# Attention scores in 128-row matmuls: a zero-padded query tile for the low-part product, and a split in two parts for group C of the second layer

## The chip, the cores and the metric

One core of one Trainium2 chip runs the whole program. The metric is the device time of one execution in microseconds; for the kernel before it is the median of three runs. The engines are TensorE (PE in the profile, PEld for its weight loads), VectorE (DVE), ScalarE (ACT), GpSimd (POOL) and SyncE (SP).

## The reference, cut to what matters

Two transformer layers over 256 latent and 256 context tokens, then a third block (recurrent mixer, cross attention, feed-forward) on the latent tokens. Everything is float32. Each of the two layers has three groups of attention heads; the change touches their scores.

```python
def attention(q, k, v, bias_or_mask, sink):          # for every head
    s = einsum('qd,kd->qk', q, k) * scale + bias_or_mask
    p = softmax(concat([s, sink]))                    # sink: group B only
    return p @ v
# group A: 8 heads of 64 columns, neighbourhood bias on the latent keys
# group B: 12 query heads, 4 key heads of 64 columns, band mask, a sink
# group C: 6 heads of 192 columns: 128 wide ones (keys from a low-rank product)
#          and 64 with rotary embedding, shared by the heads on the key side
# latent queries read 512 keys (latent and context), context queries 256 (context)
# layer 1: queries of both streams; layer 2: latent queries only
```

## The kernel before

**Parts and products.** A float32 value is kept as two float32r parts, a high and a low one, each exact in a one-pass product. An input product is the sum of three one-pass products, high x high, low x high, high x low (lines 416 to 418, and 436 to 439 for transposed results). Weights come from DRAM as raw tiles (`raw`, on SP's queue), ACT makes the high part (line 372) and DVE the low part (line 373). Products of plain float32 operands are also possible; they take several passes.

**Scores of 64 columns.** For groups A and B and for the rotary columns of group C, `stacked` transposes the queries of a pair of heads and puts, for each head, the high part in one half of the 128 partitions and the low part in the other half (`Q`). For the keys it puts the high part in both halves (`KK`), and the low parts of the two heads of a pair in the two halves of a tile of its own (`KL`). One product over 128 rows then gives (high + low) x high; a second one, over the 64 rows of the head's half alone, adds high x low. In the trace these two are `Ss<-k,q` (128 rows) and `Ss<-kl,q` (64 rows), both at line 525 in `scores`.

**Group C.** Its 128 wide columns are transposed by `toT`. With `parts=1` the result is one float32 tile (`T`), copied by ACT or DVE (`copy`, lines 360 to 368), and the wide part of a score is one float32 product `Ss<-T,T`. With `parts=2`, `toT` calls `split_scaled`: ACT writes the high part, DVE the low part, and `job_c` makes three one-pass products. `nparts = 1, 1` chooses one part in both layers.

**Jobs.** `scores` writes one PSUM bank for one head and 128 queries; DVE adds bias or mask and takes the maximum (lines 530, 532), ACT makes the exponentials (line 536), `divide` scales them (line 546), `turn` transposes them on PE (line 553) and `values` multiplies them with the values (line 568, out of a pair's four score tiles). These are stages of a job: `first`, `part`, `second`, `end`. `job_ab` and `job_c` push the jobs; for group A's latent queries a stage `load` ahead of `first` fetches the bias on SP's queue and POOL adds a mask to it (line 992).

**Order.** The stages run between the steps of the input and output products. `tick` counts microseconds of PE's work; `serve` starts a new job every `every` = 2.0 of them, and a number between two stages (`soft`, `lag`, `lag2`, `ahead`) is the least distance between them. Norms of heads are `urgent` work: a square on ACT, a sum on DVE, a power on POOL (`rstd`, line 351), then the scaling. The rotary embedding ends in an addition on POOL (line 729). DVE also has side work in layer 1, sums for the modulation vectors (line 664, `ada_steps`). The framework orders the instructions of an engine by when they can run and by the order in which they were written; each engine then goes through its list in order.

**Memory.** 50 tiles `U` of 128x512 hold activations; 40 tiles of 16 columns hold small sums (`small`). A tile `cs` holds constants for the whole program; its last 256 columns, `tri` and `stri`, are used by the third block alone (`exps`, line 1514).

Of the kernel before, what the change touches and what calls it, by code (L numbers as in the profile page):

```python
# [25 lines left out]
# per-partition vectors: name -> (first column, columns)  # L26
# [25 lines left out]
# constants that depend on shapes alone: name -> (first column, columns)  # L52
# [13 lines left out]
def flip():  # L66
    """reverses 64 by 64"""
    p = np.arange(128)
    return ((p[:, None] // 64 == p[None] // 64) & (p[:, None] % 64 == 63 - p[None] % 64)).astype(np.float32)
# [28 lines left out]
# weights as blocks of two k-tiles [128, 2 x columns] in the order of their use: name -> (rows, chunks), a chunk  # L98
# being [(first column, columns)] side by side
# [20 lines left out]
# shift and scale of the first layer: (first k-tile, k-tiles) of the parts that are worked out one after another  # L120
# [12 lines left out]
def packed_ada(w):  # L133
    """the parts of PARTS as [k-tile, 128, shift and scale]; then the gate of the first layer, shift and scale and the
    gate of the second as [quarter of the channels, block, 128 columns, 512 channels]"""
# [7 lines left out]
class Weights:  # L143
    """a packed weight in DRAM"""
# [14 lines left out]
class Act:  # L159
    """Transposed activations [channel, token] as two float32r parts, 512 // T k-tiles to a unit; make(u) works  # L160
    out unit u when it is first needed (or one unit ahead of that)."""
# [21 lines left out]
class Pair:  # L183
    """Token tiles 0, 1 of one and 2, 3 of another."""
# [8 lines left out]
class K:  # L193
    # microseconds of the tensor engine: between the starts of two jobs, two urgent stages, two stages of a job; between
    # the halves of a norm, from norms to transposes, from these to the jobs; from scores to the division, to the
    # transposes, to the values; from the load of a bias to the scores
    every, spaced, gap = 2.0, 0.65, 1.3
    settle, hold, after, soft, lag, lag2, ahead, split_lag, unit_lag = 4.0, 6.5, 2.5, 1.2, 2.5, 3.0, 2.5, 1.2, 2.0
    nparts = 1, 1

    def __init__(self, ctx, tc, a):
# [14 lines left out]
        self.cs = self.const.tile([128, NCS], F32, name="cs")  # L216
        nc.scalar.dma_start(self.cs, a["cst"])
# [9 lines left out]
    # ---- tiles  # L227
# [4 lines left out]
    def c(self, name):  # L232
        a, n = CS[name]
        return self.cs[:, a:a + n]
# [11 lines left out]
    def B(self, name, tag=None, bufs=2, cols=512, dt=F32):  # L246
        """a tile of the pool of the part at hand"""
        return self.bp.tile([128, cols], dt, name=self.name(name), tag=tag or name, bufs=bufs)
# [5 lines left out]
    def small(self, n=16):  # L254
        return self.sm.tile([128, 16], F32, name=self.name("sm"), tag="s", bufs=40)[:, :n]

    # ---- work that runs beside the products: jobs of several stages (a number is a delay after the stage before it),
    # or a number alone, before the next start),
    # which start one after another when the urgent work that was there before them is done
# [3 lines left out]
    def urge(self, f, ts, then=()):  # L263
        """f(t), a generator that yields once, for all ts, then the stages then; before the jobs that follow"""
# [11 lines left out]
    def free(self):  # L276
        """whether the next job may start"""
# [33 lines left out]
    def defer(self, dt, f):  # L311
        """f, which waits for another engine's work, dt later"""
        self.late.append((self.now + dt, f))

    def catch_up(self, all=True):
        """before what needs deferred work"""
# [28 lines left out]
    # ---- elementwise helpers  # L345
    def rstd(self, ss, n, count):
        """(ss / count + eps) ** -0.5 for [128, n]"""
# [6 lines left out]
    def copy(self, out, in_, scale=None):  # L354
        """to SBUF on ScalarE and VectorE by turns; scale: an AP [128, 1] or a number"""
# [14 lines left out]
    def split(self, hi, lo, src):  # L370
        """src = hi + lo, each exact in a float32r product"""
# [9 lines left out]
    # ---- products with weights from DRAM  # L381
# [3 lines left out]
    def weights(self, w, k0, pieces):  # L385
        """two k-tiles from k0 of a chunk of w: [(hi, lo)] tiles [128, <=512]"""
# [12 lines left out]
    def dense(self, act, kts, w, pieces, cols, evac, what="d", skip={}):  # L399
        """out[token, n] = act^T w for the token tiles cols, without the first skip[t] columns for tile t;  # L400
        evac(col, psum) or, for these, evac(col, psum, skip[t])"""
# [21 lines left out]
    def denseT(self, act, w, pieces, evac, what="e"):  # L423
        """out[n, token] = w^T act, tiles of 128 columns n, 512 // T to a bank; evac([bank])"""
# [18 lines left out]
    # ---- transposed activations  # L443
# [11 lines left out]
    def unit(self, T, ks, src, gain=None, rb=None, shift=None, new=None):  # L455
        """src(kt, t) -> AP [128 tokens, 128]; (hi, lo) of the transposed k-tiles ks, times gain(kt, stream) and
        the row rb, plus shift(kt, stream)"""
# [31 lines left out]
    def row(self, pt, t, r):  # L489
        """pt[p, t * 128 + i] = r[i] in every partition, for r: [128, 1]"""  # L490
# [3 lines left out]
    def rows(self, r, out):  # L494
        """r: [128, 1] of each token tile -> out[p, t * 128 + i] = r[t][i] in every partition"""
# [6 lines left out]
    def normT(self, X, gain, shift=None, ss=None, rb=None):  # L502
        """X[t][n]: [128, 512] tiles -> rms-normed, scaled and shifted, transposed; ss: their sums of squares;
        rb: the reciprocal norms as from rows()"""
# [13 lines left out]
    # ---- softmax attention  # L518
    def scores(self, qk, nk, mask=None, sink=None):
        """exponentials of the scores of one head and 128 queries, [128, nk], for divide"""  # L520
# [28 lines left out]
    def turn(self, P, nk, PT, q):  # L549
        """P transposed into PT[key pair][:, key, q*128..]"""  # L550
# [10 lines left out]
    def values(self, parts, nk):  # L561
        """parts: [(first output partition, PT, value tiles [128 keys, d])] -> psum [d.., 256 queries]"""
# [1340 lines left out]
```

## Time and profile before

| | |
|---|---|
| median of 3 runs | 3569.3 us (3567.42 to 3569.88) |
| span of the profiled execution | 3557.0 us |
| between the two | 12.3 us |
| PE busy | 3458.7 us (97%) |
| PE weight loads busy | 2943.2 us (83%) |
| DVE busy | 2295.3 us (65%) |
| ACT busy | 1787.8 us (50%) |
| POOL busy | 264.0 us (7%) |
| mean granted clock of TensorE | 0.989 of full |

The span runs from the first to the last instruction of the one execution that was profiled; the time of a run has what lies around it too. Busy shares are means over parts of the program with different limits. Layer 1's attention lies between 269 and 1000 us, layer 2's between 1278 and 1723 us, and the third block follows. A matmul's printed duration reaches into that of the next, so for PE the distance between two starts tells more than the duration.

### The profile page before, as it was taken

What the parts mean: (1) busy time and instruction counts of PE and PEld (TensorE: products, weight loads), DVE (VectorE), ACT (ScalarE), POOL (GpSimd) and SP (SyncE); (2) the same over time, 40 slices, a digit from 0 to 9 for tenths busy, and PEclk for the clock granted to TensorE, in tenths of its full rate; (3) what the DMA queues carried; (4) which work ended last, traced back from release to release, by engine and by line L of the source; (5) the groups of instructions that cost most, each with busy time, mean ns of one, the idle gap of its engine ahead of it and who ended that gap; (6) DMA issues with size and microseconds to landing.
All of it is one profiled execution on the core that took longest, in us unless ns stands there. A gap on an engine that the chain in (4) does not pass through costs nothing.

```text
span 3557.0 us, 56978 instructions
## 1 busy us (share of the span) xinstructions
PE 3458.7 (97%) x20830; PEld 2943.2 (83%) x20830; DVE 2295.3 (65%) x4925; ACT 1787.8 (50%) x3552; POOL 264.0 (7%) x315
## 2 busy tenths in 40 slices
PE   8999999999999999999999999999999899999998
PEld 3467767888777878788777999999988899999886
DVE  2359888867876555877664555555566766666554
ACT  3235555426525454666564445544555555555544
POOL 0011101101111011101110000000000000000000
PEclk9999999999999999999999999999999999999999
DMA  7645443662365434444554535555654455555665
GB/s 253 229 146 169 123 132 116 189 191 74 125 210 177 156 111 134 156 129 146 168 160 132 188 119 188 182 183 183 202 190 160 138 184 183 184 184 181 204 194 166
DMA packets 226729, 590.44 MB, mean 166 GB/s; under 512 B 39888, under 2 KB 63168, under 8 KB 226448
## 3 DMA queue, kind: packets, MB, share of 16 engines
q1 hardware_dynamic: 221104, 570.41, 50.3%
q0 software_dynamic: 4816, 15.56, 1.4%
q8 instruction: 163, 2.67, 0.3%
q14 instruction: 118, 0.97, 0.1%
q10 hardware_dynamic: 528, 0.84, 0.1%
HBM read 582.48 MB, written 4.24 MB: 165 GB/s over the span
## 4 chain that ended last, share of the span: by engine, by line
PE 91%; DVE 4%; ACT 1%; DMA 1%; issue 1%; POOL 1%; POOLq 0%; DVEq 0%; ACTq 0%; SPq 0%
PE upd L438 5%; PE upd L436 5%; PE upd L439 5%; PE Ss L525 3%; PE downd L418 2%; PE downd L417 2%; PE downd L416 2%; PE oo L568 2%; PE adao L625 2%; PE pTt L553 2%; PE L0zd L439 2%; PE L0zd L436 2%; PE L0zd L438 2%; PE L0outd L416 2%; PE L0outd L417 1%; PE L0outd L418 1%
## 5 line engine op out<-in xcount | busy, mean ns | idle before, releaser
L373 DVE TENSOR_TENSOR lo<-raw,hi 128x512 fp32r<-128x512 f32 (+3 forms) x1788 | 1200.9, 677 | 892.8 <-ACT hi L372 882.7
L372 ACT ACTIVATE hi<-raw 128x512 fp32r<-128x512 f32 (+3 forms) x1788 | 1089.4, 614 | 1314.9 <-DVE lo L373 214.6
L436 PE MATMUL upd<-hi,hi 128*128 128x256 f32 x1408 | 399.7, 284 | 0.0
L438 PE MATMUL upd<-lo,hi 128*128 128x256 f32 x1408 | 399.6, 284 | 0.0
L439 PE MATMUL upd<-hi,lo 128*128 128x256 f32 x1408 | 399.4, 284 | 0.0
L664 DVE SCALAR_TENSOR_TENSOR scr<-raw,cb 128x512 f32<-128x512 f32 x448 | 298.8, 695 | 26.2 <-DMA raw<-in_w_ada_dram 13.9
L438 PEld LDWEIGHTS upd<-lo,hi 128*128 128x128 f32 x1408 | 271.1, 193 | 0.3 <-DVE lo L480 0.3
L439 PEld LDWEIGHTS upd<-hi,lo 128*128 128x128 f32 x1408 | 271.1, 193 | 0.0
L436 PEld LDWEIGHTS upd<-hi,hi 128*128 128x128 f32 x1408 | 271.1, 193 | 0.0
L351 POOL TENSOR_TENSOR sm<-sm,mhalf 128x2 f32<-128x2 f32 (+4 forms) x116 | 116.4, 1006 | 1693.9 <-DVE sm L350 1656.5
L418 PE MATMUL downd<-hi,lo 128*128 128x512 f32 x352 | 137.0, 389 | 0.0
L417 PE MATMUL downd<-lo,hi 128*128 128x512 f32 x352 | 137.0, 389 | 0.0
L416 PE MATMUL downd<-hi,hi 128*128 128x512 f32 x352 | 137.0, 389 | 0.0
L536 ACT ACTIVATE P<-Ss,sm 128x512 f32<-128x512 f32 (+1 forms) x164 | 99.5, 607 | 66.9 <-DVE sm L532 47.3
L360 ACT ACTIVATE PT<-pTt 128x256 f32<-128x256 f32 x226 | 79.0, 380 | 76.8 <-PE pTt L553 73.2
L532 DVE TENSOR_REDUCE sm<-Ss 128x1 f32<-128x512 f32 (+1 forms) x164 | 96.1, 588 | 18.0 <-PE Ss L525 16.4
L416 PE MATMUL L0outd<-hi,hi 128*128 128x512 f32 x256 | 102.2, 399 | 4.2 <-DVE ot L1265 2.8
L436 PE MATMUL L0zd<-hi,hi 128*128 128x512 f32 x256 | 101.2, 395 | 0.0
L439 PE MATMUL L0zd<-hi,lo 128*128 128x512 f32 x256 | 100.1, 394 | 0.8 <-DVE lo L373 0.8
L417 PE MATMUL L0outd<-lo,hi 128*128 128x512 f32 x256 | 100.1, 391 | 0.0
L438 PE MATMUL L0zd<-lo,hi 128*128 128x512 f32 x256 | 100.1, 391 | 0.0
L625 PE MATMUL adao<-raw,cstat 128*32 128x512 f32 (+1 forms) x320 | 87.3, 570 | 12.5 <-DVE cstat L1335 8.7
(561 smaller groups left out, 8953.2 us busy)
## 6 DMA issues: line engine op xcount, KB each, us to landing
raw<-in_w_in_dram SPq DMA_DIRECT2D x344, 512.0 KB, 3.5
raw<-in_w_ada_dram SPq DMA_DIRECT2D x384, 256.0 KB, 3.2
raw<-in_ffn_w_up_dram SPq DMA_DIRECT2D x176, 512.0 KB, 3.5
raw<-in_w_out_dram SPq DMA_DIRECT2D x104, 512.0 KB, 3.9
raw<-in_ffn_w_down_dram SPq DMA_DIRECT2D x88, 512.0 KB, 4.2
raw<-in_w_proj_b_dram SPq DMA_DIRECT2D x32, 512.0 KB, 3.6
raw<-in_w_in_dram SPq DMA_DIRECT2D x32, 288.0 KB, 3.2
raw<-in_w_proj_a_dram SPq DMA_DIRECT2D x16, 512.0 KB, 4.3
```

What stands on the lines that cost most here:

```text
L351: nc.gpsimd.tensor_tensor(r, ms, self.mhalf[:, :n], op=OP.pow)
L372: self.nc.scalar.activation(hi, src, AF.Copy)
L373: self.nc.vector.tensor_sub(lo, src, hi.bitcast(F32))
L416: nc.tensor.matmul(ps[t][:, a], lhsT=xh, rhs=hi[:, a], start=first, stop=False)
L417: nc.tensor.matmul(ps[t][:, a], lhsT=xh, rhs=lo[:, a], start=False, stop=False)
L418: nc.tensor.matmul(ps[t][:, a], lhsT=xl, rhs=hi[:, a], start=False, stop=last)
L436: nc.tensor.matmul(p, lhsT=hi[:, s], rhs=xh, start=kt == 0 and c % per == 0, stop=False, skip_group_check=True)
L438: nc.tensor.matmul(p, lhsT=hi[:, s], rhs=xl, start=False, stop=False, skip_group_check=True)
L439: nc.tensor.matmul(p, lhsT=lo[:, s], rhs=xh, start=False, stop=kt == nk - 1, skip_group_check=True)
L525: nc.tensor.matmul(S[:, :nk], lhsT=a, rhs=b, start=i == 0, stop=i == len(qk) - 1, skip_group_check=True)
L625: nc.tensor.matmul(acc[q:q + 32, :W], lhsT=cst[:, kt, :], rhs=raws[b], start=kt < 2, stop=kt >= NKT - 2, skip_group_check=True)
L664: nc.vector.scalar_tensor_tensor(self.temp("scr"), raw, 1.0, st[s], op0=OP.mult, op1=OP.mult, accum_out=st["p"][:, s, k, q:q + 1])
```

## The change

The low-part product of a score no longer takes the 64 rows of the head's half from `Q` and `KL`. A new stage `prepare`, 0.8 of the schedule's microseconds ahead of `first`, copies the high half of the query tile (64 partitions x 128 queries) on POOL into one of two tiles for that half whose other half was set to zero once; the product then runs over all 128 rows of `KL`. `nparts` becomes 2 for the second layer, so that its group C has its wide parts split and multiplied in three one-pass products. `every` goes from 2.0 to 1.9. To make room, `tri` and `stri` leave the tile `cs` and are loaded on POOL's queue when the mixer starts, and 38 small tiles stand for 40. The comments are gone too; those lines are left out here.

```diff
-    every, spaced, gap = 2.0, 0.65, 1.3
+    every, spaced, gap = 1.9, 0.65, 1.3
+    padding = 0.8
-    nparts = 1, 1
+    nparts = 1, 2
...
-        self.cs = self.const.tile([128, NCS], F32, name="cs")
-        nc.scalar.dma_start(self.cs, a["cst"])
+        n = CS["tri"][0]
+        self.cs = self.const.tile([128, n], F32, name="cs")
+        nc.scalar.dma_start(self.cs, a["cst"][:, :n])
...
-        return self.sm.tile([128, 16], F32, name=self.name("sm"), tag="s", bufs=40)[:, :n]
+        return self.sm.tile([128, 16], F32, name=self.name("sm"), tag="s", bufs=38)[:, :n]
...
+    def padded_tiles(self):
+        self.padded, self.pad_at = {}, [0, 0]
+        for h in range(2):
+            for i in range(2):
+                t = self.padded[h, i] = self.B(f"pad{h}{i}", bufs=1, cols=128, dt=F32R)
+                self.nc.vector.memset(t.bitcast(F32), 0.0)
+
+    def pad(self, x, h):
+        t = self.padded[h, self.pad_at[h]]
+        self.pad_at[h] ^= 1
+        r = slice(64 * h, 64 * h + 64)
+        self.nc.gpsimd.tensor_copy(t[r], x[r].bitcast(F32))
+        return t
...
 # job_ab
+            def prepare(hd, q):
+                t = 2 * s + q
+                Qz[hd, q] = self.pad(Q[g, hd][:, t * 128:t * 128 + 128], (hd // 3 if g == "b" else hd) % 2)
...
-                r = slice(kv % 2 * 64, kv % 2 * 64 + 64)
-                P[hd, q] = self.scores([(x, KK[g, kv][:, ks]), (x[r], KL[g, kv // 2][r, ks])], nk, **kw)
+                P[hd, q] = self.scores([(x, KK[g, kv][:, ks]), (Qz.pop((hd, q)), KL[g, kv // 2][:, ks])], nk, **kw)
...
-                    st += [lambda hd=hd, q=q: first(hd, q), self.soft, ...
+                    st += [lambda hd=hd, q=q: prepare(hd, q), self.padding, lambda hd=hd, q=q: first(hd, q), self.soft, ...
...
 # job_c
+            def prepare(q):
+                Qz[q] = self.pad(Q["cr", hd][:, (2 * s + q) * 128:(2 * s + q) * 128 + 128], hd % 2)
...
-                                    (z, KK["cr", hd][:, ks]), (z[r], KL["cr", j][r, ks])], nk)
+                                    (z, KK["cr", hd][:, ks]), (Qz.pop(q), KL["cr", j][:, ks])], nk)
...
-            self.push(lambda: first(0), self.soft, ...
+            self.push(lambda: prepare(0), self.padding, lambda: first(0), self.soft, ...
...
 # block1, after the gains
+            self.padded_tiles()
...
 # mixer, first in its pool
+        self.cs2 = self.B("cs2", bufs=1, cols=256)
+        nc.gpsimd.dma_start(self.cs2, a["cst"][:, CS["tri"][0]:])
...
-                                 rhs=self.cs[:, CS["tri"][0]:CS["tri"][0] + 256], start=True, stop=True,
+                                 rhs=self.cs2, start=True, stop=True,
```

## Rows read from the trace of the kernel before

**Rows 1.** The page: busy us, share and count of each engine; last chain by engine.
```profile
PE 3458.7 (97%) x20830; PEld 2943.2 (83%) x20830; DVE 2295.3 (65%) x4925; ACT 1787.8 (50%) x3552; POOL 264.0 (7%) x315
...
PE 91%; DVE 4%; ACT 1%; DMA 1%; issue 1%; POOL 1%; POOLq 0%; DVEq 0%; ACTq 0%; SPq 0%
```

**Rows 2.** Busy time by stretch: stretch, length, engines' busy us (count), clock, DMA.
```profile
269.00:682.00 413.00, 405.14 (x2064) 304.15 (x2063) 351.94 (x1054) 222.00 (x574) 43.93 (x42) 1.00 0.46 139
...
1574.00:1723.00 149.00, 145.05 (x837) 119.96 (x836) 112.42 (x284) 90.56 (x190) 21.81 (x27) 1.00 0.47 151
...
545.00:607.00 62.00, 59.63 (x298) 44.16 (x296) 55.70 (x182) 36.50 (x104) 3.32 (x5) 1.00 0.40 118
```

**Rows 3.** Score tile Ss on PE: count, ns min/median/max, first and last start, forms.
```profile
L525 PE MATMUL Ss<-kl,q x156: 378/493/503, 289.8 to 1721.0; 64*128 64x512 f32 x104, 64*128 64x256 f32 x52
...
L525 PE MATMUL Ss<-T,T x72: 377/592/697, 859.3 to 1720.2; 128*128 128x512 f32 x48, 128*128 128x256 f32 x24
```

**Rows 4.** Timeline of PE, a score of 512 keys: start us, us, instruction.
```profile
289.27 0.39 PE L418 MATMUL L0vbd<-hi,lo 128*128 128x512 f32 x1
289.50 0.39 PE L525 MATMUL Ss<-k,q 128*128 128x512 f32 x1
289.81 0.50 PE L525 MATMUL Ss<-kl,q 64*128 64x512 f32 x1
290.24 0.50 PE L416 MATMUL L0vbd<-hi,hi 128*128 128x512 f32 x1
290.57 0.39 PE L417 MATMUL L0vbd<-lo,hi 128*128 128x512 f32 x1
290.80 0.39 PE L418 MATMUL L0vbd<-hi,lo 128*128 128x512 f32 x1
```

**Rows 5.** Timeline of PE, a score of 256 keys, and plain 256-column products.
```profile
451.82 0.28 PE L525 MATMUL Ss<-k,q 128*128 128x256 f32 x1
452.03 0.38 PE L525 MATMUL Ss<-kl,q 64*128 64x256 f32 x1
452.34 0.50 PE L439 MATMUL L0zd<-hi,lo 128*128 128x512 f32 x1
452.67 0.39 PE L436 MATMUL L0zd<-hi,hi 128*128 128x512 f32 x1
...
2802.18 0.28 PE L438 MATMUL upd<-lo,hi 128*128 128x256 f32 x1
2802.30 0.28 PE L439 MATMUL upd<-hi,lo 128*128 128x256 f32 x1
```

**Rows 6.** Timeline of PE, a score of group C in the second layer.
```profile
1612.86 1.02 PE L525 MATMUL Ss<-T,T 128*128 128x512 f32 x2
1613.32 0.80 PE L525 MATMUL Ss<-k,q 128*128 128x512 f32 x1
1614.05 0.49 PE L525 MATMUL Ss<-kl,q 64*128 64x512 f32 x1
```

**Rows 7.** Tile T, 1574 to 1725 us: a copy on DVE, as rows 3.
```profile
L368 DVE TENSOR_SCALAR T<-toTs,vt x1: 751/751/751, 1662.2 to 1662.2; 128x512 f32<-128x512 f32 x1
```

**Rows 8.** Timeline of PE, last pair of group C; in brackets the wait before.
```profile
1711.18 0.66 PE L758 MATMUL sts<-ident,kc 128*128 128x128 f32 x4 [1.00 <-ACT T L364]
```

**Rows 9.** POOL's groups of instructions: count, busy us, mean ns, idle before.
```profile
L351 POOL TENSOR_TENSOR sm<-sm,mhalf 128x8 f32<-128x8 f32 x20 | 35.6, 1788 | 283.3 <-DVE sm L350 283.2
L992 POOL TENSOR_TENSOR H<-H,cs 128x256 f32<-128x256 f32 x32 | 27.2, 850 | 362.3 <-DMA H<-in_rp_dram 221.5 <-DVE lo L373 69.3 <-DVE sm L532 25.2
...
masks.py:197 POOL MEMSET ident<- 128x128 f32 x1 | 0.2, 204 | 0.3 <-POOLq L1892 0.3
```

**Rows 10.** Timeline of POOL, a bias addition.
```profile
299.08 1.12 POOL L992 TENSOR_TENSOR H<-H,cs 128x256 f32<-128x256 f32 x1 [2.06 <-DVE sm L532]
```

**Rows 11.** Timeline of DVE at the same time.
```profile
298.93 0.68 DVE L664 SCALAR_TENSOR_TENSOR scr<-raw,cb 128x512 f32<-128x512 f32 x1
...
299.61 1.14 DVE L664 SCALAR_TENSOR_TENSOR scr<-raw,cb 128x512 f32<-128x512 f32 x1
```

More of the change, by code (lines that the diff above doesn't have):

```diff
@@ L233, in c @@
         a, n = CS[name]
+        if a >= CS["tri"][0]:
+            return self.cs2[:, a - CS["tri"][0]:a - CS["tri"][0] + n]
         return self.cs[:, a:a + n]
@@ L980, in job_ab @@
             k0, nk, kts = keys(s)
-            PTs, P, Hs = {}, {}, {}
+            PTs, P, Hs, Qz = {}, {}, {}, {}
             def load(hd, q):
@@ L1034, in job_ab @@
                     st = [lambda hd=hd, q=q: load(hd, q), self.ahead] if g == "a" and s == 0 else []
-                    st += [lambda hd=hd, q=q: first(hd, q), self.soft, lambda hd=hd, q=q: part(hd, q), self.lag, lambda hd=hd, q=q: second(hd, q)]
+                    st += [lambda hd=hd, q=q: prepare(hd, q), self.padding, lambda hd=hd, q=q: first(hd, q), self.soft, lambda hd=hd, q=q: part(hd, q), self.lag, lambda hd=hd, q=q: second(hd, q)]
                     self.push(*st, *([self.lag2, end] if hd % 2 and q else []))
@@ L1039, in job_c @@
             k0, nk, kts = keys(s)
-            j, po = hd // 2, hd % 2 * 64
-            st, P = {}, {}
+            j = hd // 2
+            st, P, Qz = {}, {}, {}
+            def prepare(q):
+                Qz[q] = self.pad(Q["cr", hd][:, (2 * s + q) * 128:(2 * s + q) * 128 + 128], hd % 2)
             def first(q):
@@ L1045, in first @@
                 ks = slice(k0, k0 + nk)
-                r = slice(po, po + 64)
                 x, y, z = ([p[:, tt] for p in Q["c", hd]], [p[:, ks] for p in KK["c", hd]], Q["cr", hd][:, tt])
                 P[q] = self.scores([(x[0], y[0]), *([(x[0], y[1]), (x[1], y[0])] if len(x) == 2 else []),
-                                    (z, KK["cr", hd][:, ks]), (z[r], KL["cr", j][r, ks])], nk)
+                                    (z, KK["cr", hd][:, ks]), (Qz.pop(q), KL["cr", j][:, ks])], nk)
             def part(q):
@@ L1065, in end @@
                 ready.add((ct, s))
-            self.push(lambda: first(0), self.soft, lambda: part(0), self.lag, lambda: second(0))
-            self.push(lambda: first(1), self.soft, lambda: part(1), self.lag, lambda: second(1), self.lag2, end)
+            self.push(lambda: prepare(0), self.padding, lambda: first(0), self.soft, lambda: part(0), self.lag, lambda: second(0))
+            self.push(lambda: prepare(1), self.padding, lambda: first(1), self.soft, lambda: part(1), self.lag, lambda: second(1), self.lag2, end)
         def z_chunk(ct0):
```

## The prediction, made before the change was run

> **What bounds the kernel now.** I read the busy shares and the chain that ended last first, then the busy time by stretch, then the group of the score tile, and then single starts on the tensor engine. PE is busy for 97% of the span and 91% of the last chain is PE work [rows 1]. In the stretch that holds the first layer's attention groups A and B (269 to 682 us) PE is busy 405.1 of 413 us at the full clock, while DVE has 351.9 and POOL 43.9 [rows 2]. So here the time is the sum of PE's start-to-start steps: what PE no longer has to do is gained, as long as DVE, second in line, keeps up. The duration printed for a matmul (0.39 to 0.50 us) overlaps with its neighbours', so I take costs from the distance between starts.
>
> **The low-part product: what is removed.** Each of the 156 score tiles of the two layers (104 of 512 keys, 52 of 256) ends with a product over 64 rows of the array, Ss<-kl,q, between products that use all 128 [rows 3]. With 512 columns, products that follow each other in the 128-row form start 0.23 us apart (290.57 to 290.80). Around the 64-row one the steps are 0.31 (289.50 to 289.81), 0.43 (to 290.24) and 0.33 (to 290.57): 1.07 us for three products that should take 0.69 [rows 4]. That is 0.38 us too much for one score. With 256 keys: from 451.82 to 452.67 are 0.85 us for two products of 256 columns and one of 512; by the plain steps (0.12 for 256 columns, 2802.18 to 2802.30, and 0.23) it is 0.47, so 0.38 too much again [rows 4, 5]. The excess lies on both sides of the 64-row product, so it belongs to going into that form and out of it, not to its columns. The change makes it a 128-row product over the same columns, so I expect the plain steps: 156 x 0.38 = 59.3 us less, all of it on PE. By the steps' rounding it is 0.37 to 0.40 each, 58 to 62 us.
>
> **Group C's wide part in the second layer.** `nparts` goes from 1 to 2 for that layer. Its 12 scores (6 heads, 2 query tiles) each have one float32 product Ss<-T,T, which stands in the trace as two records. From its first record to the 64-row product are 1.19 us (1612.86 to 1614.05); without the 0.31 of Ss<-k,q this is 0.88 [rows 4, 6]. Three one-pass products take 3 x 0.23 = 0.69, so 0.19 is saved, 12 x 0.19 = 2.3 us. The price is that the operands are split: for each of 3 pairs of heads, two key tiles of 512 columns and two query pieces of 256 get a DVE subtraction in addition. DVE's own copy of such a tile takes 0.75 us [rows 7], so it is at most 12 x 0.75 = 9 us of DVE in a stretch in which it is busy 112.4 of 149 us [rows 2]: hidden by PE work. Where the cover is gone is the last pair, where PE already waits 1.0 us for the copy of a key tile (1711.18) [rows 8]. The subtraction comes after that copy. Ends 0 and 1.5, I take 1 us lost.
>
> **The padded query tiles: what is added.** 156 copies of 64x128 on POOL, which has no such row. The nearest are a memset of 128x128 with 0.20 us and the bias addition on 128x256 with two inputs with 0.85 [rows 9]. I take 0.3, since the copy has one input and fewer elements than the addition: 47 us of POOL in all, on an engine that is 11% busy in the stretch [rows 2]. It costs in two ways.
>
> First, DVE. A bias addition on POOL ran from 299.08 for 1.12 us, and the DVE operation that began at 299.61 took 1.14 us instead of the 0.68 of the same operation just before [rows 10, 11]. So DVE can lose up to 0.46 us to one POOL operation. Below nothing it can't be, since the copies relieve DVE of no work. The Trainium skill ("SBUF — State Buffer", section "Who interferes with whom") states that a DVE instruction with two SBUF inputs and a GpSimd one that reads SBUF share a read interface as an exclusive lock: the later one waits for the whole of the other. By that rule a copy costs DVE at most its own length, and may itself stand behind a DVE operation; the row at 299.61 agrees with it. With 0 to 0.46 us for each of the 80 copies of groups A and B (20 heads, 2 streams, 2 query tiles), DVE's 352 us become 352 to 389, while PE's 413 fall by 80 x 0.38 to 383. DVE is then 92 to 102% of it. It is tighter in single stretches: from 545 to 607 us DVE has 55.7 of 62 us now [rows 2], some 12 scores (62/413 of 80) take PE to 57.4, and DVE comes to 55.7 to 61.2. So part of the gain is given back there as PE waits for the low parts of the weights (line 373) that stand in DVE's queue behind the side work. Ends 0 and 10 us, I take 4.
>
> Second, PE waits for a new engine. The first product of a score does not need the copy, but the last one does, and behind it on PE stand the input products. The copy needs the high part of the query (there since the pair's stage, at least one pair ahead) and its tile free again. There are two tiles for each half, so it can run as soon as the score two before it is done, about one score ahead: 413/80 = 5 us on average. It stands in POOL's order behind additions and powers, of which the longest take 1.79 us [rows 9], and behind bias loads' additions that wait for DMA. With POOL busy 11% of the time some 17 of 156 copies find it busy, for 0.9 us on average: 15 us of lateness, most of it inside the lead. Ends 0 and 18 (ten of the twenty 1.79 us powers passed on in full), I take 3.
>
> **The rest, at nothing.** `every` from 2.0 to 1.9 starts the jobs closer together; the work is the same, and PE is the bound. Four memsets on DVE before the first weights arrive, 38 small tiles instead of 40. The columns tri and stri go from the first load on ACT's queue to a load on POOL's queue at the start of the mixer; it goes ahead of the mixer's other small loads there. SP's queue gets nothing new. Each of these is within 2 us either way.
>
> **Sum.** 59.3 + 2.3 - 4 - 3 - 1 = 53.6 us. The profiled span of 3557.0 us [rows 1] becomes 3503.4; the median of the runs is 3569.3, 12.3 above that span, and what lies around the span stays. Predicted: 3569.3 - 53.6 = 3515.7 us.
>
> **Rivals.**
> A. DVE becomes the bound in the first layer's groups and POOL is often late: both losses at their upper ends, 61.6 - 10 - 18 - 1.5 = 32 us gained, 3537 us. For it speaks how near DVE's 55.7 of 62 us is to full; against it that the side work of DVE is spread over the products and PE hardly waits now.
> B. The copies come onto the path. If a copy runs only just ahead of its score (because the order on POOL puts it behind that score's neighbours), PE stops at the last product of each score. The change turns into a loss from 61.6/156 = 0.39 us of waiting per score; at the 0.85 us of the bias addition it is 156 x 0.85 = 133 us, 3569.3 - 61.6 + 133 = 3640 us. Against it: two tiles for each half, and scores that stand microseconds apart.
> C. The excess is not the 64-row form's but that of any last product of a score, or of a load of weights that comes late. Then only the 2.3 us remain and the losses eat them: 3567 to 3573 us. Against it: the product before it, also the first into its bank, starts 0.23 us after its predecessor (289.27 to 289.50) as any other [rows 4], and the step after the 64-row product is long whatever follows.
>
> **How the numbers follow.** Forecast 0.70, A 0.20, C 0.06, B 0.04. Range 3504 (62 us, the second layer's 2.3 and a little from closer jobs, nothing lost) to 3542 us (A with the lower end of the removed cost); it leaves out B, C and the tail of A. Differences under 0.2% (7 us) can't be told from no change here. Faster: forecast, A and a little of C, 0.91; same 0.05; slower 0.04.
>
> **What would show it.** Right: Ss<-kl in the 128-row form, 0.23 us (512) and 0.12 us (256) from start to start around it, three Ss<-T,T of one pass in the second layer. For A: DVE above 95% from 269 to 670 us, PE waits for line 373's low parts of several us. For B: PE waits for POOL's copies in the list of waits, tens of us. For C: the long steps are still there beside 128-row products. The forecast is wrong if PE's waits in the two layers grow by more than 25 us.

## The result, and the profile after

The changed kernel took 3525.0 us (median of 4 runs, 3521.77 to 3530.28), the kernel before 3568.4 us (4 runs, 3562.14 to 3569.88). The ratio is 0.9886, 95% interval 0.9872 to 0.9901. By the medians that is some 43 us less, by the ratio 41 (35 to 46); 53.6 us less had been forecast, and 3504 to 3542 us was the range. Lines of the code moved: 416 to 418 are now 420 to 422, 372 and 373 are 376 and 377, 525 is 529, 664 is 668, 992 is 1012; the copy is line 763, the split of `T` lines 810 (high) and 811 (low), its transposes line 826.

The same part of PE's timeline as [rows 4] and [rows 5], in the profile of the changed kernel (start us, us, instruction):

```profile
288.33 0.39 PE L422 MATMUL L0vbd<-hi,lo 128*128 128x512 f32 x1
288.55 0.40 PE L529 MATMUL Ss<-k,q 128*128 128x512 f32 x1
288.79 0.40 PE L529 MATMUL Ss<-kl,pad 128*128 128x512 f32 x1
289.02 0.39 PE L420 MATMUL L0vbd<-hi,hi 128*128 128x512 f32 x1
289.25 0.39 PE L421 MATMUL L0vbd<-lo,hi 128*128 128x512 f32 x1
...
296.86 0.28 PE L529 MATMUL Ss<-k,q 128*128 128x256 f32 x1
296.98 0.28 PE L529 MATMUL Ss<-kl,pad 128*128 128x256 f32 x1
297.10 0.40 PE L420 MATMUL L0vbd<-hi,hi 128*128 128x512 f32 x1
```

Every step around the low product is now the plain 0.23 us for 512 columns and 0.12 for 256. From 288.55 to 289.25 are 0.70 us, where 1.07 stood before. The group of the score tile (as [rows 3]) shows the new form for all 156, and `Ss<-T,T` with 84 records where 72 stood:

```profile
L529 PE MATMUL Ss<-kl,pad x156: 274/393/765, 288.8 to 1679.6; 128*128 128x512 f32 x104, 128*128 128x256 f32 x52
...
L529 PE MATMUL Ss<-T,T x84: 377/397/628, 836.7 to 1679.1; 128*128 128x512 f32 x60, 128*128 128x256 f32 x24
```

The two layers run from the first product of `L0vbd` to the first of the third block, `glrd`: 258.4 to 1809.1 us before, 256.2 to 1767.9 after. The busy time by stretch (as [rows 2]) over them, before:

```profile
258.00:1809.00 1551.00, 1507.08 (x7819) 1213.52 (x7820) 1157.09 (x2999) 796.15 (x1807) 202.52 (x224) 0.99 0.47 147
```

and after:

```profile
256.00:1768.00 1512.00, 1457.67 (x7833) 1216.10 (x7833) 1159.54 (x3009) 794.35 (x1810) 260.38 (x381) 0.99 0.49 151
```

PE's busy time fell by 49.4 us and its idle time grew by 10.4 (43.9 to 54.3). So the stretch is 39.0 us shorter. I then summed, over every two products in a row, the distance of their starts less the plain step for their columns:

| excess over the plain steps in the two layers, us | before | after |
|---|---|---|
| the three steps around each of the 156 low products | 80.2 | 20.5 |
| other input and output products, steps longer than plain by over 0.45 us | 22.6 | 32.6 |
| other input and output products, all shorter excesses | 30.9 | 38.0 |
| transposes, value products, norms and the rest | 79.4 | 80.3 |
| plain steps of the split's 12 more records (12 x 0.23) | 0 | 2.7 |

The sum falls by the same 39.0 us. The first line has the removed term: 59.7 us less. For the 120 scores outside group C alone it fell from 53.9 to 8.3 us, which is 0.38 each. About 18 us came back beside it, 17 of them in steps of input and output products, which the change doesn't touch.

A part of these 18 us is the clock. In the two layers TensorE's granted clock was at its lower level, 1.2 GHz, for 19.8 us before and for 32.7 us after. Two products of 512 columns in such a stretch of the changed kernel:

```profile
530.83 0.63 PE L420 MATMUL L0cqd<-hi,hi 128*128 128x512 f32 x1
531.26 0.63 PE L421 MATMUL L0cqd<-lo,hi 128*128 128x512 f32 x1
```

The step is 0.43 us there, where it is 0.23 at the full clock, so of each microsecond at the lower level about half is excess. By this estimate some 6 of the 18 us are the clock's. The waits of PE in the profile after (tile and line that waited, releaser; us in total, times, longest):

```profile
PE L0cqd L421 <- DVE lo L377: 3.9, 2, 3.2
...
PE toTs L826 <- DVE T L811: 3.1, 4, 1.9
PE L0outd L420 <- DVE ot L1290: 3.0, 2, 1.6
PE pTt L557 <- DVE PT L370: 2.6, 3, 1.9
PE Ss L529 <- ACT P L540: 2.2, 4, 1.2
PE sts L778 <- DVE T L811: 1.8, 1, 1.8
PE pTt L557 <- DVE P L550: 1.7, 4, 0.5
```

No row names POOL's copies. The first was 2.3 us before; the two that name `T L811` are new: they come with the split. Taken in order, every copy was done at least 2.6 us before the product that read it, half of them more than 12 us.

The third block took 1758.4 us in this profile and 1747.9 in that of before, with the same instructions. The busy time by stretch of its first 150 us, before and after:

```profile
1809.00:1959.00 150.00, 145.03 (x684) 116.94 (x683) 86.47 (x159) 85.45 (x163) 10.03 (x10) 0.93 0.46 144
```

```profile
1768.00:1918.00 150.00, 145.38 (x657) 116.39 (x656) 83.72 (x154) 82.39 (x158) 10.03 (x10) 0.88 0.44 136
```

The granted clock (third from the right) was 0.93 and then 0.88 of full: more of the stretch ran at the lower level, 1.2 GHz, and PE got through 27 fewer products in the same 150 us. What it did before the clock fell, in the profile after (timeline, and the busy time of the stretch that followed):

```profile
1847.82 0.48 PE L1580 MATMUL sgs<-sgb,ones 1*128 1x128 f32 x2
1850.20 0.49 PE L1582 MATMUL sgs<-sgw,vs 128*128 128x128 f32 x2 [1.90 <-POOL vs L1570]
...
1851.40:1882.00 30.60, 30.60 (x82) 21.50 (x81) 4.95 (x7) 4.31 (x7) 0.42 (x1) 0.50 0.16 51
```

Products of 128 columns, some of one row, and a wait of 1.90 us for POOL; then 30.6 us at half the clock, in which PE was never idle. Before, the same products and a wait of 1.91 us led to 13.7 us at half. Over the whole third block the lower level lasted 51.5 us before and 68.8 after. Less half of that, by the same estimate, the block takes 1722 and 1724 us: the clock accounts for most of the 10.5 us.

So the profiled span fell only from 3557.0 to 3526.3. The before profile was also a quick execution of its kernel: a run's time is 1.7 us above its span (3528.03 and 3526.3 in the changed kernel's profiled run), so it was one of about 3558.7 us. That is why the medians show 43 us and the spans 30.7. The clock goes with it: over 39 runs of the kernel before, spans were 3569.6 us on average where the mean granted clock was 0.985, and 3560.4 where it was 0.989, as in the profiled one.

### The profile page after: what moved, and what is told of

The parts are those of the page before. It is cut to its first block, busy times and chain, and to the rows that moved or that the text cites. A ratio compares the mean times of both kernels' runs of the same rounds, so it can differ in the third digit from the quotient of the medians.

```text
span 3526.3 us, 57200 instructions
## 1 busy us (share of the span) xinstructions
PE 3420.2 (97%) x20842; PEld 2952.3 (84%) x20842; DVE 2299.7 (65%) x4939; ACT 1785.4 (51%) x3554; POOL 321.7 (9%) x472
## 4 chain that ended last, share of the span: by engine, by line
PE 54%; issue 12%; DVE 4%; ACT 1%; POOL 1%; DMA 1%; POOLq 0%; SPq 0%; DVEq 0%; ACTq 0%
PE upd L442 5%; PE upd L440 5%; PE upd L443 5%; PE downd L420 2%; PE downd L422 2%; PE downd L421 2%; PE L0outd L420 1%; PE L0outd L422 1%; PE L0outd L421 1%; PE Ss L529 1%; DVE lo L377 1%; PE oo L572 1%; PE vd L420 1%; PE vd L422 1%; PE vd L421 1%
## 5 line engine op out<-in xcount | busy, mean ns | idle before, releaser
L422 PE MATMUL L0outd<-hi,lo 128*128 128x512 f32 x256 | 99.3, 391 | 0.2 <-DVE lo L377 0.2
```

Source lines behind the costliest of these rows:

```text
L422: nc.tensor.matmul(ps[t][:, a], lhsT=xl, rhs=hi[:, a], start=False, stop=last)
```

## Experiments

Each kernel was timed beside the kernel before; ratios are against that one. For the profiles I give the length of the two layers (from the first `L0vbd` to the first `glrd`; 1550.7 us before, 1511.7 in the changed kernel), of the second layer's group C within it (from the first `L1qcd`; 245.3 and 247.2), and of the third block. A second profile of the changed kernel (last experiment) has 1509.3 and 247.3 us; differences of some 2 us in the layers between single profiles can't be told from none.

**The 64-row form put back.** The changed kernel, with copies and split, but the product takes only the 64 rows of the head's half:

```diff
-  (Qz.pop((hd, q)), KL[g, kv // 2][:, ks])
+  (Qz.pop((hd, q))[r], KL[g, kv // 2][r, ks])      # r: the head's 64 rows, written out; job_c the same
```

> The changed kernel, with the copies, the split, the closer jobs and all else, but the low product again over 64 rows (the half of the padded tile that holds the high part). The direct price of the 64-row form where all else is the same. If the 0.38 us of each of 156 scores lies on the path: 59 us slower than the changed kernel, 3584 us, slower than before too, since the changed kernel's other parts then show as a loss of some 15 us. If a part of the excess was hidden beside DVE's work: 40 to 45 us slower, 3565 to 3570 us.

3562.3 us, ratio 1.0003 (0.9994 to 1.0013): the whole gain is gone. That is 37 us above the changed kernel's 3525.0, less than both expected values; in the profile the layers took 1561.5 us, 49.8 more, and the third block 15.4 less (1743.0). The long steps are back, on both sides of the 64-row product, although the operand is now a tile of its own that POOL filled (PE's timeline of this kernel):

```profile
289.48 0.39 PE L529 MATMUL Ss<-k,q 128*128 128x512 f32 x1
289.80 0.50 PE L529 MATMUL Ss<-kl,pad 64*128 64x512 f32 x1
290.22 0.50 PE L420 MATMUL L0vbd<-hi,hi 128*128 128x512 f32 x1
290.56 0.39 PE L421 MATMUL L0vbd<-lo,hi 128*128 128x512 f32 x1
```

1.08 us for three products, against 0.70 with 128 rows. Rival C falls with that: position in the score, operands and weight loads are the same, and only the number of rows differs. The Trainium skill ("TensorEngine Tiling (Array Packing)", section "Key Properties") says that changing the tiling mode drains TensorE. The profile prints this product's form as 64*128 where its neighbours have 128*128, which agrees; that a drain is what the 0.38 us consist of is not shown.

**Only the form.** The kernel before with the whole query tile and the whole low tile in the low product, no copies, no split, `every` at 2.0. This adds a product of the query's low part with the other head's low keys, which the reference doesn't have:

```diff
-  (x[r], KL[g, kv // 2][r, ks])
+  (x, KL[g, kv // 2][:, ks])      # job_c the same
```

> The kernel before with one edit: the low product takes all 128 rows of the query tile and of KL (each score also gets the product of the query's low part with the other head's low key part); no copies, one part in group C, jobs every 2.0. The change of form alone. Taking the changed kernel back to 64 rows cost 39 us where the excess between starts sums to 60 us. If a fixed part of that sum comes back as waits for DVE and ACT (the chain from scores to transposes keeps its length while PE's steps shrink), this gains 40 to 45 us, 3520 to 3525 us. If the rest of the change is what takes it back, this gains the whole 57 to 60 us, about 3507 us.

3516.4 us, ratio 0.9857 (0.9836 to 0.9878): 51 us less (44 to 59), between the two expected values. In the profile the layers took 1509.0 us. Nothing was added to any engine, and still only 41.7 of 60 us arrived in the layers (the profiled run of the kernel before was a quick one, so profiles show less than medians). By the same sum as above, the three steps fell from 80.2 to 27.9 us, and the long steps of the other input and output products rose from 22.6 to 29.3. So most of what came back in the changed kernel's profile isn't the price of the copies.

**No copies, stages kept.** The changed kernel with the stage `prepare` in its place, but instead of a copy it hands over the whole query tile (the same extra product):

```diff
-  Qz[hd, q] = self.pad(Q[g, hd][:, t * 128:t * 128 + 128], ...)
+  Qz[hd, q] = Q[g, hd][:, t * 128:t * 128 + 128]      # job_c the same
```

> The changed kernel with its stage prepare and its distance of 0.8 us kept, but empty: nothing is copied, and the 128-row product takes the whole query tile (each score also gets the product of the query's low part with the other head's low key part). Against the run without copies and without the stage (3532.9 us, 8 us slower than the changed kernel, which both theories had missed), this tells the copies from the order of the jobs. If the order makes those 8 us (Theory 3: moving `first` by 0.8 us shifts which wait ends last), this one is at the changed kernel's 3522 to 3525 us. If the copies' absence did it, through POOL running ahead, it is at 3530 to 3534 us too.

3518.8 us, ratio 0.9861 (0.9839 to 0.9883). That is below both expected values. The layers took 1510.2 us, 1.5 less than in the changed kernel's first profile and 0.9 more than in its second; single stretches agree with the first within 0.5 us except four (0.8 to 1.6). The profiled run was 16 us shorter than the changed kernel's, and 15.4 of these stand in the third block: 1743.0 us, with a clock of 0.97 in its first 150 us:

```profile
1766.00:1916.00 150.00, 145.43 (x707) 117.97 (x705) 88.95 (x162) 88.43 (x168) 10.05 (x10) 0.97 0.48 151
```

**No copies, stages left out.** As the last, but without `prepare` and the 0.8 us ahead of `first`:

```diff
-  st += [lambda hd=hd, q=q: prepare(hd, q), self.padding, lambda hd=hd, q=q: first(hd, q), ...
+  st += [lambda hd=hd, q=q: first(hd, q), ...      # and x in place of Qz.pop((hd, q)); job_c the same
```

> The changed kernel without the padded tiles' copies: the 128-row low product takes the whole query tile (high part in its half, low part in the other), so each score also gets the product of the query's low part with the other head's low key part, which the reference does not have. PE's work is the same as in the changed kernel, POOL loses 156 copies of 0.38 us. Theory 2 (the copies or the order on POOL take back 10 to 20 us of the gain): 3505 to 3515 us. Theory 1 (no product ever waits for a copy; DVE is slowed by 0.02 us per overlapped operation): 3523 to 3527 us, within the noise of the changed kernel.

3532.9 us, ratio 0.9915 (0.9902 to 0.9928): slower than the changed kernel, with less work; both theories missed it. The layers took 1520.3 us. Between this and the last kernel there is no difference in instructions, only in when jobs start. The waits moved: `L0zd` for low parts of weights from 1.2 to 2.2 us, `pTt` for `P` from 1.5 to 2.0, while `L0cqd` for low parts fell from 4.0 to 2.8. The lower clock lasted 27.7 us of the layers there and 41.3 here, so that by the estimate above some 7 of the 10 us are the clock's. An order of jobs was worth 10 us in the layers, clock included, more than the copies.

**The split.** The changed kernel with `nparts` back at 1, 1, and the kernel before with `nparts` 1, 2 alone:

```diff
-    nparts = 1, 2
+    nparts = 1, 1
```

> The changed kernel, with group C of the second layer back in one float32 part (nparts 1, 1); the padded 128-row product stays. In the changed kernel's trace the stretch from the start of the last layer's first query product of group C (1520.7 us) to the start of the third block (1767.9) takes 247.2 us, as against 245.2 before, although its 12 scores should be 12 x 0.38 + 2.3 = 6.9 us shorter. Theory 1 (the split costs there, through PE's transposes that wait for DVE's low parts): this stretch falls to about 241 us, the whole to about 3520 us. Theory 2 (the copies on POOL take the gain back, there as elsewhere): the stretch grows by the 2.3 us of the three-pass products, 249 us, the whole about 3527 us.

3518.7 us, ratio 0.9874 (0.9861 to 0.9887); group C of the second layer 244.7 us, which is 2.5 less than with the split and between the two values expected.

> The kernel before with one edit: nparts 1, 2, the split of the second layer's group C alone. By the sum of the prediction 2.3 us less on PE and 1 us more at the last pair, 1 us faster. By the run with one part (4 us faster than the changed kernel) it costs 2 to 5 us: 3567 to 3570 us, with PE's waits for the copies T of 2 us each in the stretch of group C.

3567.7 us, ratio 1.0005 (0.9993 to 1.0017): no difference in the time, which lies in the expected range, and waits for `T` of 1.0 to 2.3 us. In the profile the stretch grew from 245.3 to 250.3 us. Five microseconds are 0.14%, inside that interval. And the split taken from the kernel without copies:

> The changed kernel with the stages of the padding kept but without the copies on POOL (the low product takes the whole query tile, so the product of the query with the other head's low part is added to the scores, which the reference doesn't have), and with layer 2's group C unsplit again. Theory 1: the split costs 4 to 5 us in its own stretch and the copies nothing; then this kernel stands 4 to 6 us below the one without copies but split (3518.8), at 3513 to 3515, and level with the kernel before with only the full-row form (3516.4) within 4 us. Theory 2: the split costs nothing that lasts and the 6 us between the changed kernel and the unsplit one were order; then it is at 3517 to 3521.

3516.9 us, ratio 0.9871 (0.9853 to 0.9889), between the values of the two theories; the stretch took 244.2 us against 249.5. So in three pairs of profiles the split cost 2.5, 5.0 and 5.3 us in its stretch, where 1.3 us of gain was forecast. In the time the pairs differ by 6.3 (3525.0 and 3518.7), 0 and 1.9 us; none of these is beyond the intervals, so the loss is shown in the stretch and not in the total. Over all profiles with 128-row products the stretch took 245.8 to 249.9 us with the split (five profiles) and 244.2 to 244.7 without (four). The mechanism can be read in the timelines. In the changed kernel, at the second pair:

```profile
1598.87 0.38 PE L826 MATMUL toTs<-ident,qc 128*128 128x128 f32 x2
...
1599.48 0.46 ACT L810 ACTIVATE T<-toTs,gt 128x256 fp32r<-128x256 f32 x1
...
1600.17 0.69 DVE L668 SCALAR_TENSOR_TENSOR scr<-raw,cb 128x512 f32<-128x512 f32 x1
...
1600.78 1.46 DVE L377 TENSOR_TENSOR lo<-raw,hi 128x512 fp32r<-128x512 f32 x2
...
1602.17 0.47 DVE L811 SCALAR_TENSOR_TENSOR T<-toTs,gt,T 128x256 fp32r<-128x256 f32 x1
...
1602.69 0.44 PE L826 MATMUL toTs<-ident,qc 128*128 128x128 f32 x2 [1.92 <-DVE T L811]
```

and with `nparts` 1, 1:

```profile
1598.39 0.38 PE L826 MATMUL toTs<-ident,qc 128*128 128x128 f32 x2
...
1599.00 0.46 ACT L368 ACTIVATE T<-toTs,gt 128x256 f32<-128x256 f32 x1
...
1599.51 0.44 PE L826 MATMUL toTs<-ident,qc 128*128 128x128 f32 x2
```

`toT` writes a PSUM tile out of two that scores and transposes share. With one part, ACT's copy frees it at 1599.5. With two parts it is free only when DVE has made the low part too, and that stands behind a side sum and two weight subtractions; ACT's part was done at 1599.9, DVE's at 1602.6. PE waits 1.92 us. At the last pair it waits for `T L811` again (1.8 us, for the transposes `sts`; 1.0 before, for ACT's copy [rows 8]), and there the granted clock is 0.5 for 6.8 us from 1670.4 on. In the five profiles with split and 128 rows this stretch at half lasted 6.8 or 10.2 us, in the four unsplit ones 3.4. In all of group C the lower clock lasted 12.0 to 17.4 us in the five and 5.3 to 8.7 in the four, which by the estimate above is about 3 us, nearly all of the difference between them; in the kernel before with the split it explains 1 of the 5 us. That the waits bring the lower clock is likely from their order in time, not shown.

**DVE's side work halved in one stretch.** The stretch of `L0cqd` gained almost nothing (62.3 us before, 62.0 after), though its 10 scores should have brought 3.8 us (the expectation below counts 13). It has the longest wait for a weight's low part in the layers that grew. The rows of PE and DVE there, in the changed kernel:

```profile
525.79 0.61 PE L420 MATMUL L0cqd<-hi,hi 128*128 128x512 f32 x2
526.14 0.94 DVE L668 SCALAR_TENSOR_TENSOR scr<-raw,cb 128x512 f32<-128x512 f32 x1 [1.48 <-POOL ro L733]
...
527.62 0.68 DVE L668 SCALAR_TENSOR_TENSOR scr<-raw,cb 128x512 f32<-128x512 f32 x1
...
528.23 0.68 DVE L902 TENSOR_TENSOR b<-b,sm 128x512 f32<-128x512 f32 x1
528.83 1.28 DVE L377 TENSOR_TENSOR lo<-raw,hi 128x512 fp32r<-128x512 f32 x2
529.57 0.50 PE L421 MATMUL L0cqd<-lo,hi 128*128 128x512 f32 x1 [3.16 <-DVE lo L377]
```

DVE itself idles 1.48 us for the rotary addition on POOL, then goes through side sums before the low part that PE needs. The edit gives that stretch half the rate of side sums:

```diff
-  self.rates = dict(..., cq=0.2, ckv=0.2, c=0, out=0.2)
+  self.rates = dict(..., cq=0.1, ckv=0.2, c=0, out=0.2)
```

> The changed kernel, with DVE's side work at half the rate beside the first layer's product cq (0.1 instead of 0.2 steps per us; four steps are done later). That product gained 0.3 us where 13 scores promise 4.9; PE waits there for 3.9 us for a weight's low part. Theory (DVE binds in this stretch): cq takes 57 to 58 us instead of 62.0, the whole is 3 to 4 us faster unless the steps bind later. Rival (the waits there come from the order and not from DVE's load): cq stays at 61 to 62 us.

3524.1 us, ratio 0.9882 (0.9869 to 0.9895): no gain. The stretch took 61.5 us with 16 side sums in it in place of 31, and that of `L0outd` grew from 223.0 to 228.2; that the sums left over fell due there is the likely reason, not a shown one. Two other profiles say what the stretch lost. In the second profile of the changed kernel it took 60.4 us with the same wait of 3.16 us: in the first, the clock was at half for 3.4 us from 530.3 on, right after that wait, and 1.6 us are its price. With the form alone (the second experiment) the same 276 PE instructions took 58.4 us beside 29 side sums, so there the whole 3.8 us arrived. DVE's load is no floor in this stretch.

**Longer distances.** The unsplit kernel with more time between the stages of a job:

```diff
# values of three lines, shortened
-    every = 1.9     soft, lag, lag2 = 1.2, 2.5, 3.0      nparts = 1, 2
+    every = 1.85    soft, lag, lag2 = 1.4, 2.9, 3.4      nparts = 1, 1
```

> The changed kernel with layer 2's group C unsplit again and with longer planned distances between the parts of one unit's job (1.2, 2.5 and 3.0 us become 1.4, 2.9 and 3.4) and new jobs a little more often (1.9 becomes 1.85). Theory 1: what came back of the 60 us came back because the shorter products bring the next part of a unit onto TensorE before VectorE and ScalarE have made its operand; longer distances then take the waits for P, PT and T out (in the changed kernel the gaps of TensorE above 0.45 us between 256 and 1810 us sum to about 52), and the time falls 3 to 6 us below the unsplit kernel's 3518.7, to 3513 to 3516, with gaps below 45 us. Theory 2: the waits come from the order in which jobs happen to meet on VectorE and ScalarE; another set of distances only moves them, and the time stays at 3517 to 3524 with gaps of 45 to 60 us.

3522.3 us, ratio 0.9874 (0.9857 to 0.9891), layers 1508.5 us, idle times of PE over 0.45 us between 256 and 1810 us 47.4 in sum (45.7 in the changed kernel): the rival's values. Waits of `pTt` for `PT` fell from 2.6 to 1.8 us and those of `Ss` for `P` rose from 2.2 to 3.0. Longer distances move the waits and don't remove them.

**The changed kernel once more**, to see whether the third block's slow stretch was an accident of one execution:

> The changed kernel once more, beside the others on one chip, as their base. In its first profile TensorE was at half its clock for 120.6 us in all, as against 80.1 in the profile before and 80 to 100 in the other runs; 30.7 of them were one stretch from 1851 us, in the third block, whose instructions the change does not touch. If that is a matter of the single execution, this profile has another sum there and the third block takes 3 to 10 us less, and the median is again 3522 to 3528 us.

3525.2 us, ratio 0.9875 (0.985 to 0.99): the median as expected. The slow stretch came again (30.7 us at the lower clock from 1847.5, third block 1760.9 us), so there my expectation was a miss. But it isn't the changed kernel's own: the longer distances gave the same 30.7 us and a third block of 1758.6, while the same part lasted 6.8 us in the unsplit kernel (third block 1748.7), in the one with the stages kept but no copies (1743.0) and in that with 64 rows (1743.0). Over the whole third block the lower clock lasted 32.9 to 74.8 us in the twelve profiles; less half of that, by the same estimate, the block takes 1720 to 1727 us in every one. So its spread is the clock's, and not the change's. What decides the clock is open.

## Why the prediction came out as it did

**What bounds the kernel, and the low-part product: right.** PE's steps set the time, and the 64-row form cost what its starts showed: 59.3 us forecast, 59.7 gone. The form put back took the whole gain away; that is shown, not argued.

**The gain that arrives: too large by a quarter.** The step that failed is the one from the sum of PE's steps to the end. The prediction passed the 59.3 us on in full and let losses come only through the copies (4 us by DVE, 3 by POOL) and the last pair (1 us). They came without any copies: the form alone brought 41.7 of 60 us in the layers, 51 by the medians. Part of it is a term that the prediction doesn't have, TensorE's clock: by the estimate from the steps some 6 of the 18 us that came back in the first profile of the changed kernel, and some 3 in the second, where the lower clock lasted 26.1 us of the layers. The rest are waits. PE now reaches its next operand earlier, while the chain behind a score (DVE's maximum, ACT's exponentials, DVE's scaling, the transposes) and the low parts of the weights take as long as before; so the long steps of its input and output products grow by 10 us and the short ones, clock included, by 7. The prediction had seen a place: it named 545 to 607 us, and the stretch of `L0cqd`, which overlaps with it, gave most of its gain back, by DVE's low parts behind side work and by the clock. But halving the side work there didn't bring it back, with the form alone the gain arrived there, and longer distances between the stages didn't help either. What is shown is that two kernels with the same instructions in another order differ by 10 us in the layers; that what came back in waits is of this kind, and not a floor set by the chains, is argued and stays open. The prediction's own sign of being wrong, waits of PE that grow by more than 25 us, did not appear: its idle time grew by 10.4. And the 7 us taken off for copies that cost next to nothing stood in for a loss of another kind; that the total was only 10 us off is in part luck.

**Copies on POOL: forecast 7 us, found 0 to 3.** With copies the layers took 1511.7 and 1509.3 us, without 1510.2; with one part in group C 1510.0 with and 1507.4 without. That is about what two profiles of one kernel differ by. The group of the copies in the profile after (busy us and mean ns, then idle before them):

```profile
L763 POOL CAST pad<-q 64x128 fp32r<-64x128 f32 x156 | 57.7, 377 | 404.7 <-PE Ss L529 321.4 <-ACT q L790 51.6 <-ACT q L792 18.5
```

A copy took 0.38 us (0.3 assumed) and waited mostly for the score that had its tile before, as forecast. The 0.46 us that a DVE operation was feared to lose came from a bias addition [rows 10, 11]. POOL and DVE around a copy, both from the changed kernel:

```profile
289.25 0.83 POOL L763 CAST pad<-q 64x128 fp32r<-64x128 f32 x1 [11.06 <-PE Ss L529]
...
297.39 0.29 POOL L763 CAST pad<-q 64x128 fp32r<-64x128 f32 x1 [1.17 <-PE Ss L529]
297.72 1.27 POOL L1012 TENSOR_TENSOR H<-H,cs 128x256 f32<-128x256 f32 x1
...
289.25 0.69 DVE L668 SCALAR_TENSOR_TENSOR scr<-raw,cb 128x512 f32<-128x512 f32 x1
...
298.40 1.14 DVE L668 SCALAR_TENSOR_TENSOR scr<-raw,cb 128x512 f32<-128x512 f32 x1
```

The bias addition again made a side sum take 1.14 us. Beside the copy at 289.25 it was the copy that took long, 0.83 us for 0.29, and DVE's sum took its usual 0.69. Over the 40 side sums that ran beside a copy and no other work of POOL the mean is 0.700 us, over the 340 with POOL idle 0.686; all 295 DVE operations beside a copy alone took 2.2 us more in sum than their kind with POOL idle. So a copy cost DVE about 0.01 us. The Trainium skill ("SBUF — State Buffer", section "Who interferes with whom") has the later one of the two wait for the whole of the other; the long copy agrees, and by that rule too a short copy can cost DVE only its own length. The bound of 0.46 was taken from an operation four times as long.

**The split: wrong sign.** Forecast 2.3 - 1 us; in the profiles it cost 2.5 to 5.3 in its stretch. The three one-pass products did come, 0.23 us apart, and an undisturbed score of this group fell from 1.61 us (from 1618.92) to 1.16 (from 1576.53): 0.45 for form and split together, where 0.57 was forecast. The cost was bounded by DVE's work and one wait at the last pair [rows 8]; missed was that the PSUM tile now has a second reader at the end of DVE's queue, so PE waits at every pair (0.4, 1.9 and 0.8 us in the first profile), and the lower clock that follows the longer waits. The wait at the last pair, 0.8 us longer, came as forecast.

**Rivals.** B fell: no wait for POOL's copies at all, since the tile was free early enough for every copy to be done 2.6 us or more ahead. C fell with the 64 rows. A's time (3537) is 12 us off, and its mechanism did not act: DVE's busy time in the layers is the same (1157 and 1160 us), 361 of 403 us or 90% in the first layer's groups where A asked for over 95%, and the copies cost next to nothing. Its second sign, longer waits for the weights' low parts, is there in `L0cqd` (3.9 us for 2.3) and hardly elsewhere.

**The base.** "12.3 above that span, and what lies around the span stays" was a misreading: 1.7 us lie around the span (1.7 to 3.1 in all runs on record), and the rest was that the profiled execution was quicker than the median. The forecast of the span (3503.4) was therefore 10 us too low in addition; the forecast of the median was not touched by it.

**No better version was found beyond the noise.** With what the reference asks for, the changed kernel without the split has the lowest median, 3518.7 us, 6 below the changed one; the intervals of the two ratios overlap.

## What to carry to other kernels

In a stream of 128-row products bound by TensorE, as here, a single product over half the rows costs more than a zero-padded one over all of them, and the cost shows in the starts around it and not in its duration; paying an idle engine 0.3 to 0.4 us for the padding is a good trade. Of what is taken from the bounding engine, don't count on all where it waits for chains through other engines: here 39 to 50 of 60 us arrived in the layers. Look for what is late next before looking at the price of the added work, and read the time at the lower clock in both profiles before comparing them. When a tile gets a second reader on another engine, ask when the last of the two will have read it, not how long it takes.

## What the runs showed of the hardware that had not been expected

A 64-row product among 128-row ones costs 0.38 us more than a 128-row one whatever its columns, 256 or 512. Where POOL and DVE met, the short copy on POOL paid (0.83 us for 0.29), the long addition made DVE pay (1.14 for 0.68). TensorE's granted clock fell to half mostly at the same places of the program, but for 80 to 121 us in all; the third block's same instructions took 1743 to 1761 us, the shortest in profiles with 6.8 us at half some 80 us into it, the longest in those with 30.7 us there. Less half of its time at the lower clock, it took 1720 to 1727 us in all twelve profiles (an estimate).
